# Three edits to a one-core transformer layer: pairwise squares at the start, a second job list in the attention loop, and a DRAM accumulation in one phase of the last MLP matmul

## The chip, the core and the metric

The kernel runs on one core of a Trainium2 chip. The metric is device time in microseconds (us) from the start to the end of one execution. The core has TensorE (PE, with its weight loads as PEld), VectorE (DVE), ScalarE (ACT), GpSimd (POOL) and SyncE (SP, which only issues transfers here); each runs its own instruction list in order and waits for others by semaphores.

## What is computed

One layer on x of 2048 tokens by 1024 features, all in float32, with scales, shifts and gates taken from a vector c:

```python
mod = c_act @ w_ada[l] + b_ada[l]                     # c_act = silu(c)
sh1, sc1, gt1, sh2, sc2, gt2 = split(mod, 6)
h = rmsnorm(x, g_norm1[l]) * (1.0 + sc1) + sh1
proj = h @ w_in[l]
# 8 heads of stick-breaking attention, strictly causal, 64 wide
# 8 heads of chunked softmax: own chunk of 64 and 8 chunks back, clipped relative bias
x = x + gt1 * (mixed @ w_o[l])
h = rmsnorm(x, g_norm2[l]) * (1.0 + sc2) + sh2
x = x + gt2 * (jnp.square(jax.nn.relu(h @ w1[l])) @ w2[l])   # hidden width 4096
```

## The kernel before

Everything stands in one function, `encoder_kernel`. x lies with features on the 128 partitions, in four token blocks of 512 (`TB`) and eight feature rows of 128 (`KT`). Each float32 operand of a large matmul is split into a high part (an ACT cast to the rounded type `fp32r`) and a low part (a DVE or POOL subtraction, `split`); `mm3` then makes three matmuls. A wrapper, `Ordered`, keeps the instructions of each engine in the order in which the program issues them, so the order of the code is the order on the engine; and because every call passes the wrapper's line 42, nearly all rows of the profile say L42, and instructions are told apart by the names of their tiles.

The stages, by the trace: the start up to about 20 us; projections up to about 365; attention up to about 1275; a transition with the last out-projection rows and the second norm; then the MLP from about 1340 to the end.

**The start** (lines 530 to 594). 14 `idle` matmuls run on PE (`keep_busy`) while c and block 3 of x come in. `silu(c)` is spread over the array (`cg`, then 8 matmuls into `cs`). Nine more `idle` matmuls follow. ACT squares the eight rows of block 3, the first into `nsaa3`, the others into `nsqa3_1` to `nsqa3_7`; DVE adds each of the seven to `nsaa3` in turn; then `norm_columns` makes four one-column matmuls (`pva3`) that sum over partitions. Nine `idle` matmuls more. Then DVE: a column of `mod` from the ada weights `wa8` (`ada_column`, a custom operation), `nva` (mean plus eps), POOL's power, another column from `wa0`, three small corrections into `nya`; ACT and POOL make the diagonal tiles `ndga`, PE spreads them with four matmuls into `pra`, three `idle` matmuls, and DVE scales row 0 of x (`xt`), from which `ht` and the first projection matmuls (`pq`) come.

**Attention** (the loop from line 1342). 448 steps: units of one head, one block group g of 512 queries, and (stick-breaking) one key block, four steps each, in group order 2 and 3 together, then 1, then 0. Each step issues, in this order: PE transposes of the weights of eight steps ago (`wt`); a first part of the softmax or stick-breaking (`z`, `p`, `e`, `s` tiles); the splits of those transposes (`wth`, `wtl`); a second part; the jobs that the step before has put on the list `soon`; then jobs popped from the list `heavy` (one, or two where more than three wait; in "short" steps only what exceeds three); the value matmuls into a PSUM bank `acc`; the next step's scores; and filler matmuls: projections into banks `pf` and out-projections into banks `po`. Jobs on `soon` that carry a bank (the evictions of `pf` and `po`, with casts named `stf` and `svf`) go to the end of `heavy`.

When a unit's values are complete, `finish` (line 756) goes to `heavy`: an ACT copy `otmp<-acc`, and by another `heavy` job, `rest`, the ACT copy `o<-acc`, after which the bank is free; then POOL adds the two. For the second head of a pair, `keep` (line 780) follows some steps later by `wait` (one step for each count): 6-1, 4-1, 4-1 and 2-1 steps for groups 3, 2, 1 and 0, and then through `heavy`. `keep` is a split (ACT cast, POOL subtraction) of `o` into `os` and a store into `scr_m`. `square` (line 1177) is an ACT square of a finished row of x, run from `soon`.

**The last MLP matmul** is done as seven products (Strassen's way, `OUTER` = 1, 5, 6, 3, 7, 2, 4) of eight steps of six matmuls each, in six phases; phase i = 7, 2, 5, 3, 4 are "doubled" (class `Outer`). In each step ACT and DVE split the operands (`opr`, `ol`), and DVE also makes sums `r<-r,r` for coming steps. At the end of products 5, 6, 3, 7, 2 and 4 (`Outer.end`, line 1893), for two PSUM banks each, `weigh` (line 1754) adds gate times bank to a loaded row x: one DVE operation `scalar_tensor_tensor` on `txo` or `cxo` for each of two rows, r=0 and r=1. Rows come by SP from `scr_x` (`load_x`, line 1905) and go by SP to `scr_x`, or to the output where `last` holds. In phase 5, the third doubled phase, rows with r=1 are finished and rows with r=0 are not: phases 3 and 4 read those again from `scr_x`. Elsewhere (`gather`, line 1761) a POOL transfer that adds to DRAM (`accum_op`) does such an update already, after an ACT scaling.

Of the kernel before, what the change touches and what calls it, by code (L numbers as in the profile page):

```python
# [9 lines left out]
F32 = mybir.dt.float32  # L10
# [69 lines left out]
def encoder_kernel(ctx, tc, xs, c, g1, g2, w_in, w_first, w_rest, gqk, bias, w_o, w1, w2, w_ada, b_ada, out):  # L80
# [163 lines left out]
    if True:  # L244
# [285 lines left out]
        for k in range(2):  # L530
            load_first(k)
        act.activation(ccol[:, 1], ccol[:, 0], AF.Sigmoid)
        dve.tensor_tensor(ccol[:, 1], ccol[:, 1], ccol[:, 0], op=ALU.mult)
        for i, e in ((0, dve), (KT // 2, pool)):
# [5 lines left out]
        for k in range(KT):  # L540
            pe.matmul(cs[:, k * P : (k + 1) * P], ones, cg[:, k], start=True, stop=True)
        keep_busy(9, idle)
        acc = np_.tile([P, TB], F32, tag="nsa", name="nsaa3")
        act.activation(acc, xts[3][0], AF.Square)

        def more_squares(*ks):
            for k in range(*ks):
                sq = stp.tile([P, TB], F32, tag="qh", name=f"nsqa3_{k}", bufs=6)
                act.activation(sq, xts[3][k], AF.Square)
                dve.tensor_tensor(acc, acc, sq, op=ALU.add)  # L550

        more_squares(1, KT)
        pv = norm_columns(pq, acc, "a3")
        keep_busy(9, idle)
        v3, y3, t3 = (np_.tile([P, 4], F32, tag=t, name=f"{t}a3") for t in ("nv", "ny", "nt"))
# [163 lines left out]
    if True:  # L719
# [36 lines left out]
        def finish(u):  # L756
# [13 lines left out]
            def add():  # L770
                pool.tensor_tensor(o[rows, :], o[rows, :], tmp[rows, :], op=ALU.add)
                if u.h % 2:
                    wait({3: 6, 0: 2}.get(u.g, 4) - 1, lambda: heavy.append(lambda: keep(u, o)))

            heavy.append(rest)

# [14 lines left out]
        class Unit:  # L791
# [26 lines left out]
            def values(self, j):  # L818
# [7 lines left out]
                if end:  # L826
                    soon.append(lambda: heavy.append(lambda: finish(self)))

# [339 lines left out]
        def finish_row(g, n, ps, xr):  # L1168
# [47 lines left out]
            if n == 0:  # L1216
                rows[g] = rp.tile([P, TB], F32, tag="r", name=f"r{g}")
            soon.append(square)

# [50 lines left out]
        rest = 0  # L1270
        late, soon, first, heavy = [], [], [], []

# [29 lines left out]
        def load(u):  # L1302
            need = (10,) if u.ca else (2, 3, 0, 1) + ((4,) if u.g == 0 else ())
            if u.g < 2:
                while not all((p, u.g) in have for p in need):
                    while soon or heavy:
                        (heavy or soon).pop(0)()
                    force(filler[0])
            u.load()
# [32 lines left out]
        for i in range(len(steps) + LAG):  # L1342
# [30 lines left out]
            short = front is not None and not front.ca and front.diag and fs > 1  # L1373
            for _ in range(max(0, len(heavy) - 3) if short else min(len(heavy), 1 + (len(heavy) > 3))):
                heavy.pop(0)()
            while len(late) > AVLAG:
# [6 lines left out]
        for u, j in late:  # L1383
            value(u, j)
        while soon or heavy:
            (heavy or soon).pop(0)()
        later.flush()
# [22 lines left out]
    if True:  # L1410
# [431 lines left out]
        class Outer(Step):  # L1842
# [50 lines left out]
            def end(self, n):  # L1893
# [4 lines left out]
                for b, done in {5: (("22", 0),), 6: (("12", 0),), 3: (("12", 1),), 7: (("22", 1),), 2: (("11", 1),), 4: (("21", 1),)}.get(pr, ()):  # L1898
                    for x, mb, row, odd, last in Outer.outs[b, n]:
                        weigh(x, ps, row)  # L1900
                        if done:
# [3 lines left out]
            def load_x(self, b):  # L1905
                home = kept if self.i in (5, 7) and b in ("22", "11") else temp
                for n in range(2):
                    Outer.outs[b, n] = []
                    for r, odd in {2: ((0, 1),), 3: ((0, 0),), 4: ((1, 1),), 7: ((1, 1), (1, 0)), 5: ((0, 0), (1, 0))}[self.i]:
                        mb, row = 2 - int(b[1]), HK * r + 2 * (int(b[0]) - 1) + n  # L1910
                        x = home(f"xo{self.i}_{b}_{n}{odd}")
                        sp.dma_start(x, scr_x[2 * mb + odd, row])
                        Outer.outs[b, n].append((x, mb, row, odd, self.i in (2, 3, 4) or (self.i == 5 and r > 0)))
# [255 lines left out]
```

## Time and profile before

| what | us |
|---|---|
| median of 3 runs | 2519.99 (2519.06 to 2520.8) |
| the profiled execution's own time | 2519.46 |
| its span in the trace | 2517.8 |
| PE busy | 2501.8 (99%) |
| DVE busy | 2034.4 (81%) |
| ACT busy | 1519.6 (60%) |
| POOL busy | 776.7 (31%) |
| transfers | 705.77 MB, mean 280 GB/s |

The span runs from the first to the last instruction in the trace; 1.7 us of the execution lie around it. Times inside the trace count from the span's start. A row of the timeline gives the start, the duration, the engine, the operation, "written<-read" tiles, the count of merged instructions, and in brackets the idle time just before them on that engine and what released it.

### The profile page before, as it was taken

The page shows a single profiled execution, that of the slowest core. Times are in us where ns is not written, and L with a number is a line of the kernel's source. Part 1 is how long each engine was busy: PE and PEld are TensorE (multiplying, and loading weights), DVE is VectorE, ACT ScalarE, POOL GpSimd, SP SyncE. Part 2 cuts the span into 40 slices and gives each one's busy share as a digit, 9 for nine tenths or more (in the row PEclk, how much of TensorE's full clock was granted, in tenths as well). Part 3 has the DMA queues.
Part 4 walks back from the last instruction along what each step waited for, and adds up shares of the span by engine and source line. Part 5 has one row for each costly group of instructions (what it writes and reads, how often), then busy time and mean ns, then how long its engine had stood idle before and what let it go on. Part 6 is the DMA issues. An engine that isn't in the chain of part 4 may idle for free.

```text
span 2517.8 us, 39521 instructions
## 1 busy us (share of the span) xinstructions
PE 2501.8 (99%) x12374; PEld 2096.3 (83%) x12374; DVE 2034.4 (81%) x3581; ACT 1519.6 (60%) x2916; POOL 776.7 (31%) x1162
## 2 busy tenths in 40 slices
PE   9999999999999999999999999999999999999999
PEld 8888888888888888888988888888888888888787
DVE  7656777887789888999868777779877859799998
ACT  6333424778876687666755555567555546576665
POOL 4330154776776677776720000000000000010000
PEclk9999999999999999999999999999999999999999
DMA  9879968789888788866787878996998996887882
GB/s 352 335 296 362 356 271 290 235 259 307 259 262 262 237 252 258 272 197 207 220 313 265 297 283 314 337 347 189 328 328 268 318 365 260 313 251 280 309 276 84
DMA packets 296548, 705.77 MB, mean 280 GB/s; under 512 B 32145, under 2 KB 88465, under 8 KB 284689
## 3 DMA queue, kind: packets, MB, share of 16 engines
q1 hardware_dynamic: 289856, 688.55, 80.0%
q0 software_dynamic: 5040, 9.96, 2.2%
q10 hardware_dynamic: 1440, 4.72, 0.5%
q8 instruction: 98, 1.61, 0.3%
q14 instruction: 114, 0.93, 0.1%
HBM read 476.09 MB, written 227.02 MB: 279 GB/s over the span
## 4 chain that ended last, share of the span: by engine, by line
PE 94%; DVE 3%; ACT 1%; issue 1%; DMA 1%; POOL 0%; DVEq 0%; SPq 0%; ACTq 0%; POOLq 0%
PE ps L42 28%; PE ps_s L42 16%; PE pt L42 11%; PE acc L42 7%; PE wt L42 7%; PE pf L42 6%; PE po L42 5%; PE z L42 5%; PE pq L42 3%; PE pso L42 2%; PE cz L42 2%; PE ct L42 1%; PE px L42 1%; DVE p L42 1%; DVE opr L42 0%
## 5 line engine op out<-in xcount | busy, mean ns | idle before, releaser
L42 ACT CAST wth<-wt 128x512 fp32r<-128x512 f32 (+3 forms) x544 | 257.5, 484 | 174.3 <-PE wt L42 161.6
L42 PE MATMUL ps<-h,opw 128*128 128x512 f32 x1512 | 358.6, 389 | 0.0
L42 DVE TENSOR_TENSOR wtl<-wt,wth 128x512 fp32r<-128x512 f32 (+3 forms) x544 | 291.2, 547 | 62.0 <-ACT wth L42 57.7
L42 POOL TENSOR_TENSOR b<-p 128x512 f32<-128x512 f32 (+1 forms) x320 | 292.0, 913 | 158.1 <-DVE p L42 95.7
L42 PEld LDWEIGHTS ps<-h,opw 128*128 128x128 f32 x1512 | 283.6, 188 | 58.9
L42 PE MATMUL pt<-w,ht 128*128 128x512 f32 x1248 | 288.2, 391 | 0.0
L42 PE MATMUL ps_s<-h,opw 128*128 128x512 f32 x1152 | 277.1, 389 | 0.0
L42 PEld LDWEIGHTS pt<-w,ht 128*128 128x128 f32 x1248 | 233.0, 188 | 47.7
L42 DVE TENSOR_TENSOR_SCAN p<-z,p,zero 128x512 f32<-128x512 f32 x192 | 245.3, 1279 | 24.0 <-ACT z L42 19.4
L42 PEld LDWEIGHTS ps_s<-h,opw 128*128 128x128 f32 x1152 | 216.0, 188 | 45.1 <-DVE cp L42 0.3
L42 ACT CAST opr<-r 128x512 fp32r<-128x512 f32 x280 | 174.3, 623 | 129.1 <-PE ps L42 71.3
L42 PE MATMUL acc<-wth,v 128*128 128x512 f32 (+3 forms) x544 | 221.9, 411 | 3.0 <-ACT o L42 3.0
L42 PE MATMUL ps<-opr,ol 128*128 128x512 f32 x960 | 222.0, 390 | 0.4 <-DVE opr L42 0.3
L42 PEld LDWEIGHTS ps<-opr,ol 128*128 128x128 f32 x960 | 179.8, 188 | 40.2 <-DVE opr L42 1.9
L42 ACT ACTIVATE z<-z 128x512 f32<-128x512 f32 (+1 forms) x320 | 166.7, 521 | 54.3 <-PE z L42 49.6
L42 DVE TENSOR_TENSOR opr<-r,opr 128x512 fp32r<-128x512 f32 x280 | 184.5, 681 | 10.8 <-ACT opr L42 10.1
L42 PE MATMUL acc<-wtl,v 128*128 128x512 f32 (+3 forms) x544 | 185.9, 348 | 0.0
L42 PE MATMUL z<-k,q 128*128 128x512 f32 (+3 forms) x640 | 183.3, 368 | 2.1 <-DVE p L42 2.1
L42 POOL DMA_DIRECT2D scr_x<-txu x12 | 10.5, 876 | 546.2 <-ACT txu L42 544.4
L42 PE MATMUL ps<-oph,opv 128*128 128x512 f32 x768 | 175.2, 389 | 0.3 <-DVE txo L42 0.2
L42 PE MATMUL wt<-ident,b 128*128 128x128 f32 x1088 | 170.7, 272 | 0.4 <-DVE p L42 0.4
L42 PEld LDWEIGHTS ps<-oph,opv 128*128 128x128 f32 x768 | 144.0, 188 | 31.0 <-DVE txo L42 0.6
(232 smaller groups left out, 5053.9 us busy)
## 6 DMA issues: line engine op xcount, KB each, us to landing
r<-scr_hid SPq DMA_DIRECT2D x80, 512.0 KB, 6.7
q<-scr_q SPq DMA_DIRECT2D x128, 256.0 KB, 5.2
w<-in_w_dram SPq DMA_DIRECT2D x64, 512.0 KB, 5.7
k<-scr_k SPq DMA_DIRECT2D x240, 128.0 KB, 4.4
v<-scr_v SPq DMA_DIRECT2D x120, 256.0 KB, 4.3
wa<-in_w_ada_dram SPq DMA_DIRECT2D x48, 512.0 KB, 6.2
ow<-scr_wo SPq DMA_DIRECT2D x24, 1024.0 KB, 6.3
l<-scr_t SPq DMA_DIRECT2D x20, 1024.0 KB, 7.6
```

Source lines behind the costliest of these rows:

```text
L42: return lambda *x, **y: self.tc.keep_in_program_order(f(*x, **y))
```

## The change

It has three parts.

1. At the start, each square has its own tile (`nsqa3_0` to `_7`), and DVE adds them in pairs as they come: (0,1), (2,3), (0,2), (4,5), (6,7): five additions in place of seven. The column sums add up in PSUM over three sets of four matmuls, on tiles 0, 4 and 6. The two runs of nine `idle` matmuls become one run of five, behind the column sums.
2. In the attention loop, a new list `urgent` is emptied before `heavy`. `finish` and its `rest` go to `urgent`; `keep` goes to `urgent` for groups 2 and 3 and to `heavy` for 1 and 0, after 5, 3, 3 and 2 steps for groups 3, 2, 1, 0. Evictions of `pf` and `po` stay on `heavy`, and so does `square`, which ran from `soon` before. The number of pops in a step is taken from both lists together.
3. In phase 5, rows with r=0 are neither loaded nor weighed nor stored: ACT scales the bank by the gate into a temporary tile `xa`, and POOL adds that to `scr_x` by a transfer, 1 or 3 ticks later.

```diff
@@ -529,7 +529,28 @@
 ...
+        sqs = []
+
+        def squares(*ks):
+            for k in range(*ks):
+                sqs.append(stp.tile([P, TB], F32, tag="qh", name=f"nsqa3_{k}", bufs=6))
+                act.activation(sqs[k], xts[3][k], AF.Square)
+
+        def add(a, b):
+            dve.tensor_tensor(sqs[a], sqs[a], sqs[b], op=ALU.add)
+
+        pv = pq.tile([P, TB], F32, tag="ps", name="pva3")
+
+        def into_columns(a, *flags):
+            for i in range(4):
+                pe.matmul(
+                    pv[:, i : i + 1], sqs[a][:, i * P : (i + 1) * P], ones[:, 0:1],
+                    start=flags[0] and i == 0, stop=flags[1], skip_group_check=True,
+                )
+
+        squares(2)
         act.activation(ccol[:, 1], ccol[:, 0], AF.Sigmoid)
+        add(0, 1)
         dve.tensor_tensor(ccol[:, 1], ccol[:, 1], ccol[:, 0], op=ALU.mult)
         for i, e in ((0, dve), (KT // 2, pool)):
             ks = slice(i, i + KT // 2)
@@ -539,19 +560,16 @@
             )
 ...
-        keep_busy(9, idle)
-        acc = np_.tile([P, TB], F32, tag="nsa", name="nsaa3")
-        act.activation(acc, xts[3][0], AF.Square)
-
-        def more_squares(*ks):
-            for k in range(*ks):
-                sq = stp.tile([P, TB], F32, tag="qh", name=f"nsqa3_{k}", bufs=6)
-                act.activation(sq, xts[3][k], AF.Square)
-                dve.tensor_tensor(acc, acc, sq, op=ALU.add)
-
-        more_squares(1, KT)
-        pv = norm_columns(pq, acc, "a3")
-        keep_busy(9, idle)
+        squares(2, 6)
+        add(2, 3)
+        add(0, 2)
+        into_columns(0, True, False)
+        add(4, 5)
+        into_columns(4, False, False)
+        squares(6, KT)
+        add(6, 7)
+        into_columns(6, False, True)
+        keep_busy(5, idle)
         ada_column(KT, adas[KT])
         dve.tensor_scalar(v3, pv[:, 0:4], 1.0 / D, EPS, op0=ALU.mult, op1=ALU.add)
@@ -770,9 +788,9 @@
             def add():
                 pool.tensor_tensor(o[rows, :], o[rows, :], tmp[rows, :], op=ALU.add)
                 if u.h % 2:
-                    wait({3: 6, 0: 2}.get(u.g, 4) - 1, lambda: heavy.append(lambda: keep(u, o)))
-
-            heavy.append(rest)
+                    wait({3: 5, 0: 2}.get(u.g, 3), lambda: (urgent if u.g > 1 else heavy).append(lambda: keep(u, o)))
+
+            urgent.append(rest)
 
         def wait(steps, job):
             soon.append(job if steps == 1 else lambda: wait(steps - 1, job))
@@ -824,7 +842,7 @@
                 pe.matmul(self.acc[:, cols], self.v[:, kb, :], wh[:, cols], start=self.first and j == 0, stop=False)
                 pe.matmul(self.acc[:, cols], self.v[:, kb, :], wl[:, cols], start=False, stop=end)
                 if end:
-                    soon.append(lambda: heavy.append(lambda: finish(self)))
+                    soon.append(lambda: urgent.append(lambda: finish(self)))
@@ -1215,7 +1233,7 @@
 ...
-            soon.append(square)
+            soon.append(lambda: heavy.append(square))
@@ -1268,7 +1286,7 @@
-        late, soon, first, heavy = [], [], [], []
+        late, soon, first, heavy, urgent = [], [], [], [], []
@@ -1303,8 +1321,8 @@
             need = (10,) if u.ca else (2, 3, 0, 1) + ((4,) if u.g == 0 else ())
             if u.g < 2:
                 while not all((p, u.g) in have for p in need):
-                    while soon or heavy:
-                        (heavy or soon).pop(0)()
+                    while soon or heavy or urgent:
+                        (urgent or heavy or soon).pop(0)()
                     force(filler[0])
@@ -1371,8 +1389,9 @@
                 else:
                     job()
             short = front is not None and not front.ca and front.diag and fs > 1
-            for _ in range(max(0, len(heavy) - 3) if short else min(len(heavy), 1 + (len(heavy) > 3))):
-                heavy.pop(0)()
+            n = len(urgent) + len(heavy)
+            for _ in range(max(0, n - 3) if short else min(n, 1 + (n > 3))):
+                (urgent or heavy).pop(0)()
@@ -1382,8 +1401,8 @@
             later.tick()
         for u, j in late:
             value(u, j)
-        while soon or heavy:
-            (heavy or soon).pop(0)()
+        while soon or heavy or urgent:
+            (urgent or heavy or soon).pop(0)()
@@ -1897,6 +1916,12 @@
                 for b, done in {5: (("22", 0),), 6: (("12", 0),), 3: (("12", 1),), 7: (("22", 1),), 2: (("11", 1),), 4: (("21", 1),)}.get(pr, ()):
                     for x, mb, row, odd, last in Outer.outs[b, n]:
+                        if x is None:
+                            x = temp(f"xa{self.nm}_{n}")
+                            act.activation(x, ps, AF.Identity, scale=mod[:, 5 * KT + row : 5 * KT + row + 1])
+                            to = scr_x[2 * mb + odd, row]
+                            later.add(1 + 2 * n, lambda to=to, x=x: pool.dma_start(to, x, accum_op=ALU.add))
+                            continue
                         weigh(x, ps, row)
                         if done:
                             dst = rows_of(out, mb, row, odd) if last else scr_x[2 * mb + odd, row]
@@ -1908,8 +1933,10 @@
                     Outer.outs[b, n] = []
                     for r, odd in {2: ((0, 1),), 3: ((0, 0),), 4: ((1, 1),), 7: ((1, 1), (1, 0)), 5: ((0, 0), (1, 0))}[self.i]:
                         mb, row = 2 - int(b[1]), HK * r + 2 * (int(b[0]) - 1) + n
-                        x = home(f"xo{self.i}_{b}_{n}{odd}")
-                        sp.dma_start(x, scr_x[2 * mb + odd, row])
+                        x = None
+                        if self.i != 5 or r:
+                            x = home(f"xo{self.i}_{b}_{n}{odd}")
+                            sp.dma_start(x, scr_x[2 * mb + odd, row])
                         Outer.outs[b, n].append((x, mb, row, odd, self.i in (2, 3, 4) or (self.i == 5 and r > 0)))

```

On ACT, in the attention stage near 615 us of the trace, before: `e` are exponentials of the softmax, `stf` the eviction of a projection bank, `o` the second copy out of `acc`.

```order
L42 ACTIVATE e_4_2_3_7427,cols<-s_4_2_3_7377,cols 128x640
L42 CAST stf_2_1_7429<-pf_2_1_7016 128x512
L42 CAST wth_3_3_3_7455<-wt_3_3_3_7445 128x512
L42 ACTIVATE e_4_3_0_7459,cols<-s_4_3_0_7450,cols 128x512
L42 COPY o_2_3_7391<-acc_2_3_7270 64x512
L42 CAST wth_3_3_2_7480<-wt_3_3_2_7472 128x384
L42 ACTIVATE e_4_3_1_7484,cols<-s_4_3_1_7452,cols 128x384
L42 CAST wth_3_3_1_7502<-wt_3_3_1_7495 128x256
```

And with the change:

```order
L42 ACTIVATE e_4_2_3_7420,cols<-s_4_2_3_7370,cols 128x640
L42 COPY o_2_3_7384<-acc_2_3_7263 64x512
L42 CAST wth_3_3_3_7447<-wt_3_3_3_7437 128x512
L42 ACTIVATE e_4_3_0_7451,cols<-s_4_3_0_7442,cols 128x512
L42 CAST stf_2_1_7454<-pf_2_1_7009 128x512
L42 CAST wth_3_3_2_7472<-wt_3_3_2_7464 128x384
L42 ACTIVATE e_4_3_1_7476,cols<-s_4_3_1_7444,cols 128x384
L42 CAST wth_3_3_1_7495<-wt_3_3_1_7488 128x256
```

The copy `o_2_3<-acc` and the eviction `stf_2_1<-pf` have changed places; the rows around them are the same. Seven more evictions move back by one to three slots in this way. Near 1160 us, in group 0, where `z` is a sigmoid for which DVE's scan waits, ACT has before:

```order
L42 ACTIVATE sq_6_14888<-xr_6_14387 128x512
L42 ACTIVATE z_6_0_3_2_14893<-z_6_0_3_2_14893 128x512
L42 CAST wth_6_0_1_1_14911<-wt_6_0_1_1_14900 128x512
L42 CAST os_5_0_3_14916<-o_4_0_3_14432 128x512
L42 ACTIVATE z_6_0_3_3_14922<-z_6_0_3_3_14922 128x512
L42 CAST wth_6_0_1_0_14939<-wt_6_0_1_0_14928 128x512
L42 ACTIVATE z_7_0_0_0_14945<-z_7_0_0_0_14945 128x512
L42 CAST wth_6_0_2_3_14964<-wt_6_0_2_3_14953 128x512
L42 ACTIVATE z_7_0_0_1_14970<-z_7_0_0_1_14970 128x384
```

And with the change:

```order
L42 ACTIVATE sq_6_14882<-xr_6_14380 128x512
L42 ACTIVATE z_6_0_3_2_14886<-z_6_0_3_2_14886 128x512
L42 CAST wth_6_0_1_1_14904<-wt_6_0_1_1_14893 128x512
L42 ACTIVATE z_6_0_3_3_14911<-z_6_0_3_3_14911 128x512
L42 CAST wth_6_0_1_0_14928<-wt_6_0_1_0_14917 128x512
L42 CAST os_5_0_3_14932<-o_4_0_3_14425 128x512
L42 ACTIVATE z_7_0_0_0_14938<-z_7_0_0_0_14938 128x512
L42 CAST wth_6_0_2_3_14957<-wt_6_0_2_3_14946 128x512
L42 ACTIVATE z_7_0_0_1_14963<-z_7_0_0_1_14963 128x384
```

The cast `os_5_0_3` of a finished pair stands one step later, behind the sigmoid `z_6_0_3_3` that it preceded. Four casts of group 0 move in this way, those of the softmax heads of group 0 by more rows, and four ACT squares `sq` or `r` of rows of x in groups 2 and 3 stand a few rows later than before. At the end of the attention ACT has before:

```order
L42 CAST wth_7_0_1_16661<-wt_7_0_1_16654 128x256
L42 CAST os_5_0_16665<-o_4_0_16503 128x512
L42 CAST wth_7_0_0_16681<-wt_7_0_0_16675 128x128
L42 CAST wth_7_0_5_16685<-wt_7_0_5_16677 128x384
L42 COPY otmp_6_0_16690<-acc_6_0_16585 64x512
L42 CAST wth_7_0_6_16701<-wt_7_0_6_16696 128x256
L42 CAST wth_7_0_7_16705<-wt_7_0_7_16699 128x128
L42 COPY o_6_0_16689<-acc_6_0_16585 64x512
L42 COPY otmp_7_0_16722<-acc_7_0_16671 64x512
L42 COPY o_6_0_16689<-acc_7_0_16671 64x512
L42 CAST os_7_0_16726<-o_6_0_16689 128x512
```

And with the change:

```order
L42 CAST wth_7_0_1_16654<-wt_7_0_1_16647 128x256
L42 CAST wth_7_0_0_16670<-wt_7_0_0_16664 128x128
L42 CAST wth_7_0_5_16674<-wt_7_0_5_16666 128x384
L42 COPY otmp_6_0_16679<-acc_6_0_16578 64x512
L42 CAST wth_7_0_6_16690<-wt_7_0_6_16685 128x256
L42 CAST wth_7_0_7_16694<-wt_7_0_7_16688 128x128
L42 COPY o_6_0_16678<-acc_6_0_16578 64x512
L42 CAST os_5_0_16710<-o_4_0_16492 128x512
L42 COPY otmp_7_0_16715<-acc_7_0_16660 64x512
L42 COPY o_6_0_16678<-acc_7_0_16660 64x512
L42 CAST os_7_0_16719<-o_6_0_16678 128x512
```

The cast `os_5_0` has moved from ahead of the copies for heads 6 to behind them. In phase 5, at the end of product 6, DVE has before (the tiles' names begin with a letter and the phase, which this listing leaves out: `ps_1_7_s` is the bank):

```order
L42 TENSOR_TENSOR opr_3_3_26337<-r_3_1_25729,opr_3_3_26337 128x512
L42 SCALAR_TENSOR_TENSOR txo_12_00_26182<-ps_1_7_s_26130,mod,txo_12_00_26182 128x512
L42 SCALAR_TENSOR_TENSOR txo_12_00_26184<-ps_1_7_s_26130,mod,txo_12_00_26184 128x512
L42 SCALAR_TENSOR_TENSOR txo_12_10_26186<-ps_1_7_s_26132,mod,txo_12_10_26186 128x512
L42 SCALAR_TENSOR_TENSOR txo_12_10_26188<-ps_1_7_s_26132,mod,txo_12_10_26188 128x512
L42 TENSOR_TENSOR opr_3_4_26352<-r_3_2_25755,opr_3_4_26352 128x512
L42 TENSOR_TENSOR ol_3_4_26355<-l_3_0_26202,ol_3_4_26355 128x512
L42 TENSOR_TENSOR opr_3_5_26366<-r_3_2_25755,opr_3_5_26366 128x512
L42 TENSOR_TENSOR r_7_3_26369<-r_6_3_26171,r_1_3_25677 128x1024
```

And with the change:

```order
L42 TENSOR_TENSOR opr_3_3_26326<-r_3_1_25722,opr_3_3_26326 128x512
L42 SCALAR_TENSOR_TENSOR txo_12_00_26171<-ps_1_7_s_26123,mod,txo_12_00_26171 128x512
L42 SCALAR_TENSOR_TENSOR txo_12_10_26173<-ps_1_7_s_26125,mod,txo_12_10_26173 128x512
L42 TENSOR_TENSOR opr_3_4_26344<-r_3_2_25748,opr_3_4_26344 128x512
L42 TENSOR_TENSOR ol_3_4_26347<-l_3_0_26187,ol_3_4_26347 128x512
L42 TENSOR_TENSOR opr_3_5_26358<-r_3_2_25748,opr_3_5_26358 128x512
L42 TENSOR_TENSOR r_7_3_26361<-r_6_3_26160,r_1_3_25670 128x1024
```

Two of the four weighings at a product's end are gone. On ACT, two `ACTIVATE` rows `txa5_…<-ps5_…` stand behind the casts of that step, and on POOL twelve transfers `scr_x<-txa5_…` are new, in a stretch where POOL had nothing. In all DVE has 14 instructions fewer, ACT 12 more, POOL 12 more, SP 16 fewer and PE 5 fewer; the order on PE is the same but for the start.

## The prediction

> **What bounds the kernel.** I read the page first: busy times, then the chain of work that ended last. Then PE's waits, longest in total first.
>
> ```profile
> PE 2501.8 (99%) x12374; PEld 2096.3 (83%) x12374; DVE 2034.4 (81%) x3581; ACT 1519.6 (60%) x2916; POOL 776.7 (31%) x1162
> PE 94%; DVE 3%; ACT 1%; issue 1%; DMA 1%; POOL 0%; DVEq 0%; SPq 0%; ACTq 0%; POOLq 0%
> PE acc L42 <- ACT o L42: 3.0, 2, 1.9
> PE z L42 <- DVE p L42: 2.1, 5, 0.8
> PE pva L42 <- DVE nsaa L42: 1.4, 1, 1.4
> ```
>
> PE is busy for all but 16 us (2517.8 - 2501.8), and the chain is PE's for 94%. The change removes next to no PE work, so it can only gain where PE stands still, or runs slower than it could: at the start, at `acc` waits, at `z` waits, and where DVE cannot keep up. A change on ACT, DVE or POOL is worth what PE's waits there are worth, not its own duration. I sum against the profiled execution's own 2519.46 us, which is 0.53 below the median of 2519.99.
>
> **Start: -2.0 us.** The timeline of the start shows the chain that the first part shortens.
>
> ```profile
> 7.70 2.19 ACT L42 ACTIVATE nsqa<-xt 128x512 f32<-128x512 f32 x4 [0.17 <-DMA xt<-in_xs_dram]
> 6.53 6.14 DVE L42 TENSOR_TENSOR nsaa<-nsaa,nsqa 128x512 f32<-128x512 f32 x7
> 12.73 1.05 PE L42 MATMUL pva<-ones,nsaa 128*128 128x1 f32 x8 [1.40 <-DVE nsaa L42]
> 13.64 3.68 PE L42 MATMUL idle<-ones 128*128 128x128 f32 x18
> 17.11 1.30 PE L42 MATMUL pra<-ndga,ones 128*128 128x128 f32 x8
> 18.55 0.75 DVE L42 SCALAR_TENSOR_TENSOR xt<-xt,aff,pra 128x512 f32<-128x512 f32 x1 [1.59 <-PE pra L42]
> 20.10 0.73 PE L42 MATMUL pq<-ht,wfirst 128*128 128x512 f32 x2 [1.01 <-ACT ht L42]
> ```
>
> The squares end at 7.70 + 2.19 = 9.89 and the additions at 6.53 + 6.14 = 12.67: DVE is late by 2.8, at 6.14/7 = 0.88 an addition. With pairs, four of five additions can run before the last square, and one of about 0.9 follows it: the sums stand at about 10.8, 1.9 earlier. The second loss is that `pra` was queued behind the idle matmuls (13.64 + 3.68 = 17.32): 13 fewer of them take that out, and DVE's 1.59 of waiting. The two together could bring `pq` forward by 1.9 + 1.0, the latter PE's own wait before `pq`: 2.9 at most. Against it stand the transfers, which the windows show full:
>
> ```profile
> 14.00:16.00 2.00, 2.00 (x12) 2.00 (x12) 1.90 (x6) 0.21 (x1) 1.21 (x2) 0.55 1.02 412
> 16.00:18.00 2.00, 2.00 (x13) 2.00 (x12) 0.95 (x2) 1.58 (x5) 1.46 (x4) 0.59 1.03 401
> ```
>
> DMA share is 1.02 and 1.03, at 412 and 401 GB/s, so no weight column for `mod` and no `wfirst` comes earlier; the third `mod` operation on DVE, which stands ahead of `xt`, may then wait for its transfer. I take 2.0, between 0.7 (half of the wait named `nsaa`) and 2.9. The twelve column matmuls instead of four (eight more, 1.05/8 = 0.13 each) are 1.0 of PE work in place of idle ones and hide in the gap before 12.73.
>
> **`urgent`, near 615 us: -3.1 us.** PE's longest single wait:
>
> ```profile
> 614.65 0.57 ACT L42 CAST stf<-pf 128x512 fp32r<-128x512 f32 x1
> 615.21 0.75 ACT L42 CAST wth<-wt 128x384 fp32r<-128x384 f32 x2
> 616.80 0.58 ACT L42 COPY o<-acc 64x512 f32<-64x512 f32 x1
> 617.44 0.50 PE L42 MATMUL acc<-wth,v 128*128 128x512 f32 x1 [1.93 <-ACT o L42]
> 618.00:620.00 2.00, 2.00 (x8) 1.60 (x7) 1.04 (x5) 0.00 (x0) 0.25 (x1) 0.59 1.07 280
> 620.00:622.00 2.00, 2.00 (x9) 1.81 (x8) 0.61 (x2) 1.09 (x3) 1.92 (x2) 0.55 1.03 388
> 622.00:624.00 2.00, 2.00 (x15) 1.77 (x14) 0.94 (x4) 1.40 (x5) 1.05 (x2) 1.00 0.90 353
> ```
>
> The copy that frees `acc` stood behind the eviction, a `wth` cast and an exponential. In the new order it takes the eviction's place at 614.65 and ends near 615.2; the next matmul on `acc` then waits for its `wth` cast, which ends about 615.8, not for the copy. So 617.44 becomes about 615.85: 1.6 of the 1.93. After the gap the granted clock is 0.59 and 0.55 for two windows of 2 us, with 8 and 9 matmuls in place of 15: at 0.57 for about 3.4 us PE loses 0.43 x 3.4 = 1.5. If the gap goes, that slow stretch should go too. Together 3.1, from 1.6 (the clock still falls, since PE is thinly used here) to 1.93 + 1.5 = 3.4.
>
> [...]
>
> The second `acc` wait (3.0 - 1.93 = 1.07) has the same instructions ahead of its copy as before, and stays.
>
> **Moved `os` casts, group 0: -1.2 us.**
>
> ```profile
> 1159.30 0.62 ACT L42 CAST os<-o 128x512 fp32r<-128x512 f32 x1 [1.70 <-POOL o L42]
> 1159.83 0.58 ACT L42 ACTIVATE z<-z 128x512 f32<-128x512 f32 x1
> 1160.51 1.28 DVE L42 TENSOR_TENSOR_SCAN p<-z,p,zero 128x512 f32<-128x512 f32 x1 [1.46 <-ACT z L42]
> 1161.85 0.62 PE L42 MATMUL z<-k,q 128*128 128x384 f32 x2 [0.81 <-DVE p L42]
> ```
>
> ACT stood 1.70 for POOL's addition with a ready sigmoid behind it; DVE's scan waited 1.46 for that, and PE 0.81 for the scan. One step later the sum has long been made. This wait goes, and with it most of the 2.1 listed; other waits of the list come from squares that also move behind the sigmoids. I take 1.2 (0.81 and about half of the other 1.3); ends 2.0 and, where a moved cast meets a tighter place, a loss of 1.0. The moved `stf` casts are costed at nothing: PE fills that bank again only much later (below).
>
> **End of the attention: +1.3 us.** Here the same delay costs.
>
> ```profile
> 1271.18 0.63 ACT L42 CAST os<-o 128x512 fp32r<-128x512 f32 x1
> 1273.89 0.59 ACT L42 COPY o<-acc 64x512 f32<-64x512 f32 x1
> 1343.75 0.57 ACT L42 COPY ps_s<-ps 128x512 f32<-128x512 f32 x1
> 1345.54 0.84 PE L42 MATMUL ps_s<-h,opw 128*128 128x512 f32 x3
> ```
>
> The cast of `os_5_0` now follows the copy of 1273.89, which comes 0.63 earlier without it: 1273.89 - 0.63 + 0.59 = 1273.85, 2.7 later than 1271.18. POOL's two last additions stand behind its subtraction for this tile, so they, the last store to `scr_m`, its load and the last out-projection slip by an estimated 2.4, since POOL has small gaps there. The nearest slack that I see on PE behind that chain is 1345.54 - (1343.75 + 0.57) = 1.2. What passes is 2.4 - 1.2, some 1.3; 0 if slack elsewhere takes it, 2.4 if none does.
>
> **Phase 5: -2.6 us.** In PE's timeline a product of 48 matmuls is one row or two, and starts where the bank changes.
>
> ```profile
> 2302.72 11.04 PE L42 MATMUL ps_s<-opr,ol 128*128 128x512 f32 x48
> 2313.60 11.60 PE L42 MATMUL ps<-opr,ol 128*128 128x512 f32 x48
> 2325.04 5.83 PE L42 MATMUL ps_s<-opr,ol 128*128 128x512 f32 x25
> 2337.53 7.84 PE L42 MATMUL ps<-opr,ol 128*128 128x512 f32 x31
> 2349.67 11.04 PE L42 MATMUL ps_s<-opr,ol 128*128 128x512 f32 x48
> 2275.00:2350.00 75.00, 73.82 (x317) 58.80 (x317) 75.00 (x113) 47.02 (x81) 0.00 (x0) 1.00 0.81 282
> L42 DVE SCALAR_TENSOR_TENSOR cxo<-ps,mod,cxo 128x512 f32<-128x512 f32 x8 | 5.4, 736 | 0.0
> ```
>
> An undisturbed product takes 2313.60 - 2302.72 = 10.88. The next three take 11.44, 12.49 and 12.14: 0.56 + 1.61 + 1.26 = 3.4 lost. The window says to whom: DVE 75.00 of 75, ACT 47.02, POOL nothing. The change takes two weighings of 0.74 from DVE at each product's end, 1.5 a product, about what the worst product is over. ACT gets two scalings a product, at some 0.6 as its copies above: 1.2 into 10.88 x (1 - 47.02/75) = 4.1 of room. But DVE's remaining weighing reads the bank that ACT reads first, so it may stand up to 0.65 a bank pair for ACT: I take 2.6, three quarters; ends 3.4 and, if DVE waits more than it saves, +2.0.
>
> The twelve new transfers add to DRAM from POOL's queue. Rows of the phase before, with DVE about as busy, price them:
>
> ```profile
> scr_x<-cs POOLq DMA_DIRECT2D x8, 256.0 KB, 7.2
> L42 POOL DMA_DIRECT2D scr_x<-cs x8 | 7.1, 1031 | 18.8 <-ACT cs L42 18.8
> ```
>
> 1.03 on an idle POOL and 7.2 to land. A temporary's slot (a ring of seven) is used again 14 steps later at the nearest, 14 x 10.88/8 = 19 us, and SP loads that row 16 steps later, so both are hidden. SP loses 8 loads and 8 stores; nothing waited for them.
>
> [...]
>
> **Sum.** -2.0 - 3.1 - 1.2 + 1.3 - 2.6 = -7.6; 2519.46 - 7.6 = 2511.9, and 0.5 for the median: **2512.4**.
>
> **Rivals.** (a) *Within 0.2%*: the words of the change name phase 5 only. If that alone acts, at -2.6, and what the casts gain in group 0 is lost again at the end of the attention, the time is 2517.4; with one more term, about 2515.5. For it: every ACT order gain is a single wait of this trace, and waits may reappear one tile on. Against: two of the terms, start and 615, rest on a named releaser that leaves. Chance 0.22.
>
> (b) *Slower, by late evictions*: eight bank evictions now stand behind copies and casts. One of them:
>
> ```profile
> 616.53 0.68 DVE L42 TENSOR_TENSOR stf<-pf,stf 128x512 fp32r<-128x512 f32 x1
> 633.54 0.40 PE L42 MATMUL pf<-fx,fw 128*128 128x512 f32 x1
> ```
>
> The bank is free at 617.21 and filled again at 633.54: 16 us of slack. If pops fall behind by more than that, filler matmuls stop PE with everything behind them. Priced at one longest wait each, 8 x 1.93 = 15.4 against -7.6: 2527.8. A step lasts about 2 us, and the order shows moves of one to three slots, so I give it 0.06.
>
> (c) *Slower, by transfers*: the additions to `scr_x` land later than those 19 us; the temporary's slot then holds up ACT's scaling, the `opr` casts behind it, and PE. At 30 us to land that is 11 a hold; with two slots a product the ring of seven comes round about twice in the phase: 22, against the other parts' -5.0: 2537; at 24 us to land, 2525. The 7.2 speaks against it; 0.04.
>
> **Chances and range.** Forecast 0.68, from 2508 to 2515; (a) 0.22; (b) and (c) 0.10. The lower end is -2.9 - 3.4 - 2.0 + 0 - 3.4 = -11.7, 2508.3 for the median; the upper end takes in (a) to 2518.5. A measurement tells about 0.2%, 5.0 us: faster is below 2515.0, slower above 2525.0. Faster 0.68; same 0.25, with 0.03 from the mild ends of (b) and (c); slower 0.07.
>
> **What would show it.** `pra` about 3 us earlier and `pq` near 18; no wait of 1.9 on `acc` near 615 and a granted clock of 1.0 to 622; the `z` waits on `p` under 1; the load of the last `scr_m` row some 2 later; products of 10.9 all through phase 5, DVE below 100% there, and the POOL transfers landing in 10. I am wrong if new waits on `pf`, on `xa` slots or on `ps` banks stand on PE, or if the first projection products wait for weights.

## The result, and the profile after

The median went from 2519.36 us (20 runs, 2517.09 to 2521.16) to **2514.89 us** (20 runs, 2510.7 to 2519.1): ratio 0.9981, 95% interval 0.9975 to 0.9987, or 4.5 us faster. It lies inside the range, 2.5 above the forecast of 2512.4; a drop of 7.6 was forecast. The kernel before was measured again beside each group of experiments below, with medians from 2519.36 to 2519.98; each ratio is to the one beside it. The runs of the changed kernel spread over 8.4 us, those of the kernel before over 4.1, and the profiled execution of the changed kernel took 2516.38: its trace, against that of before, accounts for 3.1 of the 4.5.

The page of the changed kernel, in the lines shown of before:

```profile
PE 2498.9 (99%) x12364; PEld 2094.8 (83%) x12364; DVE 2027.7 (81%) x3567; ACT 1526.4 (61%) x2928; POOL 787.1 (31%) x1174
PE 86%; DVE 5%; DMA 4%; ACT 2%; issue 1%; POOL 0%; SPq 0%; DVEq 0%; ACTq 0%; POOLq 0%
```

And PE's waits, as engine, tile, releaser, total us, times and longest:

```profile
PE pso L42 <- DMA opm<-scr_m: 1.9, 2, 1.6
PE cs L42 <- DVE cg L42: 1.4, 1, 1.4
PE acc L42 <- ACT o L42: 1.1, 1, 1.1
PE ps_s L42 <- ACT ps_s L42: 1.0, 1, 1.0
PE ps L42 <- DVE oph L42: 0.9, 1, 0.9
PE z L42 <- DVE p L42: 0.9, 2, 0.5
```

The totals look alike: PE still stands idle for 15.7 us of 2514.6. But three of these waits are new and come after the attention (`opm`, `ps_s<-ACT`, `oph`), and the chain has 4% of DMA where it had 1%. What was taken out in one place has come back in another. The order of PE's matmuls is the same in both kernels behind the start, so the same matmul can be looked up in both traces. Its time after less its time before gives the account (us):

| matmul at (time before) | after less before | what came in |
|---|---|---|
| 20.1, first `pq` | -0.5 | start: -0.5 |
| 623 | -4.3 | `urgent` and the clock behind it: -3.6, and -0.2 on the way |
| 1290 | -6.1 | group 0: -1.8 |
| 1303 | -3.6 | `opm` loads late: +2.5 |
| 1347 | -2.1 | ACT's copy late: +1.5 |
| 1965 | +0.6 | `oph`, `cp` late: +2.7 |
| the end | -3.05 | phase 5: -3.7 |

Near 615 us, the changed kernel's timeline of ACT and PE, and then its windows:

```profile
614.10 0.58 ACT L42 COPY o<-acc 64x512 f32<-64x512 f32 x1
614.74 0.50 PE L42 MATMUL acc<-wth,v 128*128 128x512 f32 x1
```

```profile
614.00:616.00 2.00, 2.00 (x14) 1.82 (x13) 1.76 (x8) 1.95 (x5) 0.88 (x1) 1.00 0.99 223
616.00:618.00 2.00, 2.00 (x14) 1.77 (x13) 1.52 (x8) 1.71 (x6) 1.84 (x3) 1.00 1.03 256
618.00:620.00 2.00, 2.00 (x14) 1.73 (x13) 1.78 (x6) 1.78 (x6) 1.38 (x2) 1.00 0.95 242
```

The matmul that waited 1.93 for the copy now follows it with no wait, and the granted clock (the third number from the end) stays at 1.00, where it fell to 0.59 and 0.55 before. Neither is chance: the nine traces with the new list all win 3.6 here, and in the two others that keep the old one, part 3 alone and the late split alone (both below), the wait stands and the clock falls to 0.50 behind it. In phase 5, one row of PE's timeline is a product; behind it the window, and the issues of the twelve additions (size, us to landing):

```profile
2303.35 11.04 PE L42 MATMUL ps_s<-opr,ol 128*128 128x512 f32 x48
2314.23 11.04 PE L42 MATMUL ps<-opr,ol 128*128 128x512 f32 x48
2325.11 11.04 PE L42 MATMUL ps_s<-opr,ol 128*128 128x512 f32 x48
2335.99 11.04 PE L42 MATMUL ps<-opr,ol 128*128 128x512 f32 x48
2346.87 11.04 PE L42 MATMUL ps_s<-opr,ol 128*128 128x512 f32 x48
```

```profile
2275.00:2350.00 75.00, 75.00 (x332) 62.12 (x331) 74.49 (x111) 55.26 (x95) 8.72 (x10) 1.00 0.89 294
```

```profile
scr_x<-txa POOLq DMA_DIRECT2D x12, 256.0 KB, 7.7
```

The starts are 10.88 apart four times over. The four products from 2303.35 to 2346.87 take 43.52, where those from 2302.72 to 2349.67 took 46.95. The twelve additions from POOL's queue land in 7.7.

The loss is at the end of the attention. First the kernel before: the last store of the attention's results, issued from ACT's queue, a load of 1 MB (`ow`) from SP's, and the first of SP's loads that had waited for that store to land.

```profile
1279.52 0.33 ACTq L42 DMA_DIRECT2D scr_m<-os  x1
1280.45 0.32 SPq L42 DMA_DIRECT2D ow<-scr_wo  x1
1284.00 0.33 SPq L42 DMA_DIRECT2D txr<-in_xs_dram  x1
```

The same in the changed kernel, and PE's rows behind it; then the store as the chain of work shows it (start, duration), and two windows of 5 us at the wait:

```profile
1274.37 0.32 SPq L42 DMA_DIRECT2D ow<-scr_wo  x1
1275.90 0.33 ACTq L42 DMA_DIRECT2D scr_m<-os  x1
1283.85 0.33 SPq L42 DMA_DIRECT2D txr<-in_xs_dram  x1
1296.38 0.96 PE L42 MATMUL pso<-opm,ow 128*128 128x512 f32 x3 [1.59 <-DMA opm<-scr_m]
1343.30 3.04 PE L42 MATMUL ps_s<-h,opw 128*128 128x512 f32 x12 [0.96 <-ACT ps_s L42]
```

```profile
1275.90 7.94 DMA scr_m<-os
```

```profile
1275.00:1280.00 5.00, 5.00 (x24) 4.14 (x23) 0.26 (x2) 0.00 (x0) 0.87 (x1) 1.00 0.90 296
1280.00:1285.00 5.00, 5.00 (x24) 4.14 (x23) 0.62 (x1) 0.00 (x0) 0.00 (x0) 1.00 0.14 52
```

PE and the `ow` load are 6.1 us earlier than before (1274.37 against 1280.45). The store is only 3.6 earlier, so it has changed places with the load: 0.93 ahead of it before, 1.53 behind it now. It takes 7.94 to land instead of some 4.5, and SP goes on at 1283.85 against 1284.00: nothing is won there. All that follows, the `ty` and `opm` loads, their sums on DVE, the copies on ACT, hangs on that time. The transfers are busy for the first half of that wait (DMA share 0.90) and nearly idle for the second (0.14), while SP stands for the rest of the store. One thing more stands in both traces: the load of `txr` at 1284.00 and 1283.85 reads `in_xs`, which the store doesn't write. What it waits for is a semaphore, number 100 in both, that the store raises and that the load itself raises next; SP's later loads stand behind it. What the chain would be with another semaphore was not tried. Some 430 us later DVE is still in the same place in both kernels. Before, and then after:

```profile
1715.83 1.29 DVE L42 TENSOR_TENSOR cy<-cy,r 128x512 f32<-128x512 f32 x2
1729.51 0.68 DVE L42 TENSOR_TENSOR oph<-hw,oph 128x512 fp32r<-128x512 f32 x1
```

```profile
1715.84 1.28 DVE L42 TENSOR_TENSOR cy<-cy,r 128x512 f32<-128x512 f32 x2
1729.53 0.68 DVE L42 TENSOR_TENSOR oph<-hw,oph 128x512 fp32r<-128x512 f32 x1
1730.27 2.03 PE L42 MATMUL ps<-oph,opv 128*128 128x512 f32 x6 [0.93 <-DVE oph L42]
```

PE had been 6 us ahead, and was stopped in five places (`opm` twice, `ps_s`, `oph`, `cp`) until it stood where it had stood before. In the kernel before, PE's matmul on this `oph` began at 1730.36, 0.17 after the tile was done: there was no slack to speak of.

### The profile page after: what moved, and what is told of

The parts are those of the page before. It is cut to its first block, busy times and chain, and to the rows that moved or that the text cites. A ratio compares the mean times of both kernels' runs of the same rounds, so it can differ in the third digit from the quotient of the medians.

```text
span 2514.6 us, 39505 instructions
## 1 busy us (share of the span) xinstructions
PE 2498.9 (99%) x12364; PEld 2094.8 (83%) x12364; DVE 2027.7 (81%) x3567; ACT 1526.4 (61%) x2928; POOL 787.1 (31%) x1174
## 4 chain that ended last, share of the span: by engine, by line
PE 86%; DVE 5%; DMA 4%; ACT 2%; issue 1%; POOL 0%; SPq 0%; DVEq 0%; ACTq 0%; POOLq 0%
PE ps L42 24%; PE ps_s L42 15%; PE pt L42 11%; PE acc L42 7%; PE wt L42 7%; PE pf L42 6%; PE z L42 5%; PE po L42 4%; PE pq L42 3%; PE cz L42 2%; PE ct L42 1%; DMA scr_t<-twn 1%; DMA hw<-in_w_dram 1%; DVE h L42 1%; DMA opm<-scr_m 1%
```

## The experiments

Theory A, from that reading: just behind PE runs a second chain of transfers, DVE and ACT, which starts where the last store to `scr_m` lands. That landing did not move, since the store slipped behind a load of 1 MB. Theory B: each part is worth what it saves on PE on the spot, and the waits after 1290 us are chance.

**The early split.** In the changed kernel, softmax pairs of group 0 are split one step after their sum again.

```diff
-                    wait({3: 5, 0: 2}.get(u.g, 3), lambda: (urgent if u.g > 1 else heavy).append(lambda: keep(u, o)))
+                    wait({3: 5, 0: 1 if u.ca else 2}.get(u.g, 3), lambda: (urgent if u.g > 1 else heavy).append(lambda: keep(u, o)))
```

> The changed kernel, but the split of a finished pair of softmax heads in group 0 follows after one step instead of two, as it did before the change; the stick-breaking pairs of group 0 keep two. Theory A (the chain theory): what the change won before 1270 us (6 us on PE) was mostly lost afterwards because the last store to scr_m, issued at 1275.9, landed at 1283.85, as late as before (1284.0): it had slipped behind a load of 1 MB issued at 1274.37. With the earlier split the last store is issued near 1273.5, ahead of that load, and lands near 1278 in 4.5 us; the transition starts about 6 us earlier than in the kernel before, and PE's waits on opm and on ps_s there go. Time 2510 to 2512. Theory B (each part is worth what it saves on PE on the spot, and the waits after 1290 us come from transfers that land differently from one execution to the next): no change against the changed kernel, 2514 to 2516.

Measured: 2510.41 (5 runs, 2509.89 to 2513.42), ratio to the kernel before 0.9966 (0.9954 to 0.9979), as theory A expected. The three issues in its timeline:

```profile
1273.09 0.33 ACTq L42 DMA_DIRECT2D scr_m<-os  x1
1274.02 0.32 SPq L42 DMA_DIRECT2D ow<-scr_wo  x1
1278.23 0.33 SPq L42 DMA_DIRECT2D txr<-in_xs_dram  x1
```

The store is 0.93 ahead of the load again, SP goes on at 1278.23, and PE has no wait from 1280 to 1360. One step of delay for three casts was worth 4.5 us, as much as the whole change brought. Theory B falls.

**Parts 1 and 2 alone**: the change without the edits to `Outer.end` and `load_x`.

```diff
+                        if x is None:
+                            x = temp(f"xa{self.nm}_{n}")
...
```

(These and the other lines of part 3 are left out.)

> The kernel before with parts 1 and 2 of the change alone (the start and the attention's lists), phase 5 as it was. Theory A: PE reaches the end of the attention 6 us earlier, and then waits; by 1960 us almost all is lost again. Gain 0.5 to 1.5: 2518 to 2519. Theory B: the sum of the two parts' savings less what the moved cast costs by my prediction, -0.5 - 3.6 - 1.8 + 1.3 = -4.6: 2515.

Measured: 2517.38 (11 runs), ratio 0.9994 (0.9985 to 1.0003): 2.2 by the medians, not clear of no change, and more than theory A's 0.5 to 1.5, less than half of B's 4.6. In its trace PE is 6.3 ahead at 1220 us and 0.25 at the end; SP goes on at 1283.78.

**Part 3 alone**: the kernel before with those edits.

```diff
-                        x = home(f"xo{self.i}_{b}_{n}{odd}")
-                        sp.dma_start(x, scr_x[2 * mb + odd, row])
+                        x = None
+                        if self.i != 5 or r:
...
```

> The kernel before with part 3 of the change alone (phase 5: rows that are not finished are scaled by ScalarE and added in DRAM by GpSimd's transfers). Both theories: the three slow products of phase 5 come down to 10.9 us each, -3.4: 2516. Theory A says that this is most of what the whole change brings; theory B that it is a third of what the parts save. A rival to both, that the additions from GpSimd's queue delay other transfers: -1 or less.

Measured: 2516.3 (11 runs), ratio 0.9987 (0.9978 to 0.9996), 3.3 faster as expected: of the 4.5 of the whole change, most, as theory A says. The rival was half true: in the phase the loads of 512 KB land in 7.1 instead of 4.9 and those of 1 MB in 9.4 instead of 7.3 (medians), but no wait of PE comes of it. Its products of phase 5 are 10.88 apart throughout.

```profile
2314.18 11.04 PE L42 MATMUL ps<-opr,ol 128*128 128x512 f32 x48
2325.06 11.04 PE L42 MATMUL ps_s<-opr,ol 128*128 128x512 f32 x48
```

**The late split alone**, in the kernel before:

```diff
-                    wait({3: 6, 0: 2}.get(u.g, 4) - 1, lambda: heavy.append(lambda: keep(u, o)))
+                    wait({3: 6, 0: 3}.get(u.g, 4) - 1, lambda: heavy.append(lambda: keep(u, o)))
```

> The kernel before with one number changed: the split of a finished pair in group 0 follows after two steps instead of one, through the same list. Theory A: the z waits of group 0 lose 1.5 to 2 us, but the last store slips behind the 1 MB load and lands about 4 us later than 1284, and the transition follows it: 2521 to 2523. Theory B: -1.8 for the z waits and at most +1.3 for the moved cast: 2518 to 2519.

Measured: 2520.25 (11 runs), ratio 1.0003 (0.9994 to 1.0012): between the two. The trace shows both halves. PE gains 1.2 near 1102 and 1.1 near 1161, its five `z` waits of 2.1 down to two of 0.9 in all, and loses 2.8 at 1300 and 1.4 at 1345: the store, now issued with the load, takes longest of all. (Its profiled execution was the slowest of the eleven; 1.7 us of its lag stand at the start already, whose code is unchanged.) SP's rows, and the store in the chain of work:

```profile
1280.01 0.32 SPq L42 DMA_DIRECT2D ow<-scr_wo  x1
1289.22 0.33 SPq L42 DMA_DIRECT2D txr<-in_xs_dram  x1
```

```profile
1280.09 9.11 DMA scr_m<-os
```

Is it the load that makes the store late (A1), or something else that goes with the late split, such as POOL's store some 5 us ahead (A2)? **Low parts on DVE** keeps the late split and speeds up what follows it.

```diff
-            split(os[:, 0, :], os[:, 1, :], o, pool)
+            split(os[:, 0, :], os[:, 1, :], o, dve if u.ca and u.g == 0 and u.h > 4 else pool)
```

> The changed kernel with its late split of the last softmax pairs, but the low parts of os_5_0 and os_7_0 are subtracted by VectorE, which is nearly idle there, instead of GpSimd. GpSimd's two additions then start some 1.3 us earlier and the last subtraction takes 0.7 instead of 1.3: the last store is issued near 1273.5 to 1274.2 instead of 1275.9, just ahead of the load of 1 MB at 1274.37. Theory A1 (the store is late because it stands behind that load in the 16 engines): it lands in 4.5 us, near 1278.5, and the transition follows: 2510.5 to 2512. Theory A2 (a store lands late for another reason, the store from GpSimd's queue some 5 us ahead of it): it still takes about 7.9 us, lands near 1282, and only 2 us are won: 2513. Theory B: no change, 2514 to 2516.

Measured: 2515.04 (11 runs), ratio 0.9982 (0.9973 to 0.9990), as the changed kernel. The store was issued at 1274.25, 1.65 earlier, but the load at 1274.00: it missed the place ahead of it by 0.25, and SP went on 8.3 later, at 1282.52. PE also had a new wait of 1.0 near 1275 for a row `xr` of DVE, which the expectation had not seen. The time is that of theory B, but the store did not get to where A1 wanted it, so this decides nothing between A1 and A2. So, in the changed kernel, **the load behind the store**: ow_7 is issued later in SP's order.

```diff
-                if n + 2 < KT:
+                held = g == 1 and n + 2 == KT - 1
+                if n + 2 < KT and not held:
                     ws.append(load(n + 2))
...
                 for k in range(KT):
+                    if held and k == 3:
+                        ws.append(load(n + 2))
```

> The changed kernel, with the last of the 1 MB loads (ow_7) put later in SyncE's order, behind the loads that wait for the last store to scr_m; it comes too late for PE by itself, so it is the landing of the store, not the time, that tells the theories apart. Theory A1 (the store is late because that load stands ahead of it in the engines): with nothing of that size ahead, the store, issued near 1275.9, lands in about 5 us, near 1281, and SyncE's next load of txr is issued there instead of at 1283.85. Theory A2 (the engines are late for another reason): it lands near 1284 as in the changed kernel. The time is 2513 to 2518 either way, since PE may now wait for ow_7 near 1285.

Measured: 2518.62 (10 runs), ratio 0.9996 (0.9987 to 1.0005), 0.6 above what I had allowed, with a wait of 6.0 of PE for ow_7. The landing is the point, in the chain of work and in SP's rows:

```profile
1275.06 2.97 DMA scr_m<-os
```

```profile
1278.05 1.75 SPq L42 DMA_DIRECT2D ty<-scr_x  x4
1280.84 0.38 SPq L42 DMA_DIRECT2D ow<-scr_wo  x1
```

With nothing of 1 MB ahead the same late store lands in 2.97 (I had expected about 5), though POOL's store still stands 5.3 ahead of it. A1 holds. Over all twelve traces, SP goes on 3.0 to 7.4 after the store's issue in the eight where the store is ahead of that load (before, the early split, part 3 alone, the load behind it, and the four below), and 7.9 to 9.1 after it in the four where it is behind (the changed kernel, parts 1 and 2, the late split, low parts on DVE). These ranges nearly touch, but the store comes in parts: in the trace it raises its semaphore 16 times. The eighth of these comes 2.5 to 2.9 after the issue in the eight traces and 4.7 to 6.4 in the four. That is what the order costs in these traces; how far the last part trails behind differs widely in either order.

**The start.** Three kernels on top of the early split. In the first, the sigmoid stands ahead of the squares again:

```diff
-        squares(2)
         act.activation(ccol[:, 1], ccol[:, 0], AF.Sigmoid)
-        add(0, 1)
...
+        squares(2)
+        add(0, 1)
         squares(2, 6)
```

> The kernel of the early split, with one more edit at the start: the sigmoid of c and its product stand ahead of the squares again, as before the change; pairs, the three sets of column sums and the five idle matmuls stay. Theory C (the start won only 0.5 because the sigmoid waits behind two squares, so that cs comes 0.9 later, and the 24 passes of the column sums take 2.7 us after it): cs starts near 7.3, the column sums end near 12.2 instead of 13.3, pq comes up to 1 us earlier, 18.4 to 19, and the time falls by 0.5 to 1 from 2510.4. Theory D (the granted clock decides: two stretches of 3.4 us at half speed between 12.6 and 19.4, where the kernel before had one from 14.2 to 17.6): pra still runs at half speed and pq stays within 0.4 of 19.4: 2510 to 2511.

Measured: 2509.51 (5 runs), ratio 0.9962 (0.9949 to 0.9974). `cs` started at 6.74, but the column sums ended at 13.0 and `pra` took 2.07 at a granted clock of 0.50 (windows of 1 us from 12 to 18): theory D's signs. In the second, the sums besides are made in one set:

```diff
+        keep_busy(9, idle)
...
+        add(0, 6)
+        into_columns(0, True, True)
```

> As the kernel with the sigmoid first, but the pairs are summed to one tile on VectorE (seven additions, two of them after the last square), the column sums are made once (four matmuls), and nine idle matmuls fill the time after cs again. Theory C: the column sums end near 12, as there; pq 18.4 to 19. Theory D: since PE has full-width work from 7 to 11.4 in place of one-column matmuls, the low clock lasts 3.4 us instead of 6.8, pra runs at full speed or ends half a us to 1 us earlier, and pq comes near 18.3: 2509 to 2510.

Measured: 2510.30 (5 runs), ratio 0.9963 (0.9950 to 0.9975). `pq` fits either theory, and the granted clock was 1.00 in every window of 1 us from 8 to 21 in this trace, where D expected a slow stretch. In the third, the start is that of the kernel before:

```diff
-        keep_busy(5, idle)
+        pv = norm_columns(pq, acc, "a3")
+        keep_busy(9, idle)
...
```

> The kernel of the early split, with the start of the kernel before: parts 2 and 3 of the change without part 1. Theory A and the profiles (pq at 20.10 before, 19.61 and 19.44 with part 1): 0.5 to 0.7 slower than with part 1, 2511. Rival (part 1 was worth the 2.0 that I predicted in other executions): 2512.4 or more.

Measured: 2509.79 (5 runs), ratio 0.9962 (0.9948 to 0.9976). Four starts, medians from 2509.5 to 2510.4, with 1.6 to 3.5 from the lowest to the highest run: **part 1 is worth nothing that can be told**: neither the 0.5 to 0.7 that I expected from the profiles nor its rival of 2.0. C and D stay open. `pq` came at 19.44, 19.22, 18.51 and 20.07 in the four traces; what one set of sums won, at 18.51, was lost again in the transition (+1.2 near 1340), where SP went on only 7.4 after the store, though the store stood ahead of the load. The sums in three sets, in the first of these three and in the second, one set:

```profile
9.43 3.58 PE L42 MATMUL pva<-ones,nsqa 128*128 128x1 f32 x24 [0.66 <-DVE nsqa L42]
```

```profile
12.07 1.05 PE L42 MATMUL pva<-ones,nsqa 128*128 128x1 f32 x8 [0.83 <-DVE nsqa L42]
18.51 1.19 PE L42 MATMUL pq<-ht,wfirst 128*128 128x512 f32 x4 [1.01 <-ACT ht L42]
```

**All together**: the early split, one set of sums, and the low parts on DVE; the edits are those above.

> The early split, the start with one set of column sums and nine idle matmuls, and the low parts of os_5_0 and os_7_0 on VectorE. Theory A: the last store is issued near 1271.5, some 2 us ahead of the load of 1 MB, lands before 1277, the transition's chain is no longer behind PE, and the start's 1.6 us come through: 2508 to 2509.5. Rival (from 2510 on something else holds the middle of the kernel): 2510 to 2510.5, as without the last edit.

Measured: 2510.61 (5 runs), ratio 0.9963 (0.9950 to 0.9977). The store was issued at 1272.37 and SP went on at 1277.16, as expected, and PE had no wait there; but it waited 0.9 for `oph` near 1730. The rival held: with the landing early, something in the MLP holds the next us. What sets `oph` there I did not try.

The fastest kernel of the study is the early split with the sigmoid first, 2509.51; the early split alone, with or without part 1, cannot be told from it.

## Why the prediction came out as it did

The start in the changed kernel's trace:

```profile
8.21 2.02 PE L42 MATMUL cs<-cg,ones 128*128 128x128 f32 x16 [1.39 <-DVE cg L42]
10.29 3.09 PE L42 MATMUL pva<-ones,nsqa 128*128 128x1 f32 x24
15.85 2.08 PE L42 MATMUL pra<-ndga,ones 128*128 128x128 f32 x8
19.61 1.20 PE L42 MATMUL pq<-ht,wfirst 128*128 128x512 f32 x4 [0.41 <-ACT ht L42]
```

- **Start, -2.0 predicted, -0.5 in the trace, nothing measurable in time.** The additions did end earlier (11.4 against 12.67). The step that failed is "the twelve column matmuls ... hide in the gap before 12.73". I took the eight rows of `pva` for eight matmuls; they were four, so twelve make 24 rows, 3.1 us here: the sums end at 13.38, only 0.4 earlier than before. I had also not seen that the sigmoid now stood behind two squares: `cs` began at 8.21 against 7.33. And the low clock lasted longer: the windows of 2 us from 12 to 20 show 0.68, 0.50, 0.50 and 0.61, where those of 4 us before show 0.78 and 0.80, and `pra` took 2.08 against 1.30. What of that the change brought is not shown (last section). Weights, which I had named as the limit, were not: no PE wait for a transfer stands there.
- **`urgent`, -3.1 predicted, -3.6 in the trace.** Right in its place; the slow stretch of the clock was gone together with the gap, in all nine traces with the list. That the low clock lasted about 3.4 us is what windows of 0.4 us in the kernel before show: 0.97 from 618.0, 0.50 in each from 618.4 to 621.6, 0.77 from there to 622.0 and 1.00 behind.
- **`os` casts of group 0, -1.2 predicted, -1.8 in the trace.** Right; the late split alone shows 1.2 and 1.1 at the two waits.
- **End of the attention, +1.3 predicted; +4.0 by 1347 and +6.7 by 1965 in the trace.** The failed step, and most of the miss. The slip of the store was right (2.4 estimated; PE 6.1 earlier, the store 3.6: 2.5). Two terms were wrong. I took the landing as a fixed delay, while 2.5 us of slip put the store behind a load of 1 MB, which cost 3.5 more: the chain fell behind PE by 5.9, not by 2.4. And the slack of 1.2 was read at one place, 1345.54; PE meets the chain again near 1730, where the kernel before had 0.17, so that by there the whole slip had come through. (The last 0.6 of the 6.7 is a wait on `cp` near 1962, of which the early split's trace has about half.) That PE comes 6 us earlier does no harm in itself: in the early split, with the old order of store and load, the chain moves with PE, and the terms add up (-0.7 - 3.6 - 1.8 - 3.7 = -9.8; its trace says -9.5).
- **Phase 5, -2.6 predicted, -3.7 in the trace, -3.3 alone.** Right, and all of the 3.4 came back, not three quarters, in every trace with part 3 and in none without. DVE is still busy for 74.49 of 75, but the wait for ACT's scaling that I feared is 0.1 in DVE's groups.
- **Rivals.** (a), within 0.2% because phase 5 alone acts and the casts' gain is lost again, is close to what the profiled execution did, though its reason was not chance waits but the one chain. (b) and (c) did not occur: no wait on `pf` or on a temporary's slot, and the additions landed in 7.7 with DVE busy 74.49 of 75 us beside them. One of the signs of being wrong did show, a new wait on a bank (`ps_s`, 1.0), but behind the late chain and not in phase 5.
- **The number.** That 2514.89 lies within 2508 to 2515, if only just, is in part luck. Two terms fell short by 1.5 and 5.4; three brought 0.5, 0.6 and 1.1 more than I had summed, and the median came out 1.4 better than the profiled execution. The drop of 4.5 is what rival (a) gives with one more term (2519.99 - 2515.5), and less than the 5.0 that I took for the least that a measurement tells; with twenty runs of each kernel it is still clear of no change.

Why the median (-4.5) is better than the profiled execution (-3.1), and the spread twice as wide, is only argued: in executions where the store lands sooner, part of the 6 us survives. The landing does differ: in the seven traces with the store just ahead of the load SP went on 3.9 to 7.4 after it. Parts 1 and 2 alone show the same, 0.25 in the trace and 2.2 by the medians.

## What to carry to other kernels

Gains ahead of a place where a second chain runs close behind the bound engine don't add up with the rest: read the slack of that chain at every place where the two meet, and ask what moves its start, here the landing of one store. When a step is delayed by one slot, look at the transfers on every queue that it thereby lets pass; half a step decided here between 5 and 8 us to land. See, too, whether what waits for a transfer needs its data or only its semaphore. And count rows of the profile against instructions of the program before a duration is multiplied.

## What the runs showed of the hardware that I had not expected

- A 512 KB store from ACT's queue landed in 2.97 with no large load ahead of it, and SP went on 7.9 to 9.1 after its issue where a 1 MB load from SP's queue had been issued up to 1.5 us earlier. Of the 16 parts of its landing the eighth tells the order (2.5 to 2.9 or 4.7 to 6.4 us after the issue), while the last can trail by 4.6 though the store stands ahead (one set of sums: 7.36 against 2.76). In the changed kernel the last part trails with the transfers nearly idle: DMA share 0.14 from 1280 to 1285. What holds it back was not tried.
- The granted clock at the start differed between traces of the same code. With the unchanged start, the kernel before had granted clocks of 0.78 and 0.80 from 12 to 16 and 16 to 20 us, and the late split alone, whose start is the same, had this:

```profile
12.00:16.00 4.00, 3.19 (x15) 3.19 (x16) 3.31 (x7) 0.00 (x0) 1.04 (x1) 0.63 1.03 417
16.00:20.00 4.00, 4.00 (x22) 4.00 (x21) 1.63 (x5) 1.79 (x5) 2.71 (x4) 0.52 0.98 363
```

  It reached `pq` at 21.81 instead of 20.10: 1.7 us between two traces of the same start, so one profile of each kernel doesn't settle a start here. One set of sums had 1.00 in both stretches, the same start with the low parts on DVE 0.95 and 0.62.
